# Statistics queued at other ticks, first products interleaved, last rows stored singly, and attention scores as three split-format matmuls

## The chip, the cores and the metric

The kernel runs on one core of a Trainium2 chip. The core has a matrix engine (TensorE, PE in the profile; its weight loads are shown as PEld), a vector engine (VectorE, DVE), a scalar engine (ScalarE, ACT), GpSimd (POOL) and SyncE (SP), which here only issues DMAs. Each engine takes its instructions in the order in which they stand, and waits on semaphores for others. The metric is the device time of one execution in microseconds (us); a median of several is given with their spread.

## The reference

One layer on 512 tokens of width 2048, all in float32. `rms_norm` divides by the root of the mean square over the features.

```python
xn = rms_norm(x, attn_norm_g[l])
proj = jnp.einsum("bsd,dc->bsc", xn, w_in[l])
u_val, u_gate, q, k, v = jnp.split(proj, split_pts, axis=-1)
y_conv = conformer_conv(u_val, u_gate, ...)   # GLU, conv of width 31, LayerNorm, silu
y_na = neighborhood_attention(heads(q), heads(k), heads(v), rpb[l])
mixed = jnp.concatenate([rms_norm(y_conv, conv_out_g[l]),
                         rms_norm(y_na, na_out_g[l])], axis=-1)
x = x + jnp.einsum("bsc,cd->bsd", mixed, w_out[l])
xn = rms_norm(x, ffn_norm_g[l])
up = jnp.einsum("bsd,df->bsf", xn, w_up[l])
up = depthwise_conv(up, ffn_dw_w[l], ffn_dw_b[l])
gate, val = jnp.split(up, 2, axis=-1)
x = x + jnp.einsum("bsf,fd->bsd", jax.nn.silu(gate) * val, w_down[l])
return rms_norm(x, final_norm_g)
```

The convolution and the attention have 1024 features each; the attention has 16 heads of 64, and each token of the 8 x 64 grid sees 8 x 16 neighbours. The gated MLP has 5632 hidden features.

## The kernel before

**Number format.** Activations lie with features on the 128 partitions and the 512 tokens along them. An fp32 operand is split in two fp32r parts, high and low: ACT copies the high part (`hi`), DVE subtracts it for the low one (`lo`). `mm3` makes one product of three fp32r matmuls: high by high, high by low, low by high. Weights come in units of 512 KB (eight blocks of 128 x 128): a DMA into `raw` (7 buffers), ACT to `whi` (L116), DVE to `wlo` (L117), with 4 buffers each. Every unit feeds 24 matmuls or so on PE. Not split are the attention's scores (`scores`, L449): q and k are fp32 there, and 64 partitions hold one head, so that a pair's two heads lie on the two halves of the array, taken in turn (j = 0, 1), for four blocks of tokens; the results go to four banks of two blocks each.

**Order.** The program is written as one stream, and a scheduler places each instruction by its place in the text, which `shifted` moves and `pin` fixes. Work that is to run beside a stream of products is written as generators in two lists, `steps` and `asteps`; `tick`, called after each unit of products, advances the first of each list by one `yield`. So a `yield` more or less in a generator moves the work behind it by one unit of products.

**Stages.** (1) A warm-up of PE (L231: two matmuls of 512 columns, three of 256, three of 224 on 128 rows; L235: four of 512 and eight of 256 columns on 64 rows, the two halves in turn), then the projections in an order given by `ORDER`: convolution inputs, v, and q and k per pair of heads. The depthwise convolution (`y`) runs on DVE. `attention` is a generator in `steps`: per pair of heads tables, scores, softmax, three yields, transposes on PE (`turn`, L476), and the product with v one pair later. `group_a` in `asteps`, begun at the fifth pair, is the convolution's LayerNorm: eight `ys` added (L371, L373), a matmul with ones for the mean (L376), subtraction and squares, the sum of squares (L185 in `rsqrt_steps`), then a second norm. (2) The output projection in two halves, `out_half(ma, ...)` and `out_half(mb, after)`; `after` sums into `x2`, writes it to DRAM with sums of squares, and makes of each two tiles seven combinations `comb` (`halves`, xc) for a Strassen product of two by two blocks. (3) `stats2` computes `rstd2` from those sums, in the steps of the first up products. `up_apart` (first four hidden tiles) and `up` make seven products (`pu`) each instead of eight, with weights added on DVE (`ws`); `hidden` does norm, convolution of width 3 and silu; `in_two` splits the hidden tile (hh, hl). `down` multiplies the tiles of the chunk before (`pend`) between products. Chunks are of four tiles, NCH = 11.

**rsqrt_steps.** Four one-column matmuls give column sums (st), DVE and ACT take them to 1/sqrt (rsv, rsr, rsy), DVE splits it (rsh, rsl) and makes diagonal matrices (dg), and after a `yield` PE multiplies dg with ones (L202), which spreads the result over partitions; ACT copies it from the bank (L206). Both banks have the tag "po" here, the one that `up_apart` takes for its seventh product.

**Tail.** For the last down products, three quarters of the tokens are done with features on partitions, and the last 128 tokens with tokens on partitions (`pt`). The former are normalised by `finish`, in pairs of tiles: each third pair on POOL, from a copy `rb` that ACT makes of the norm, the others on DVE; each pair is a store of 384 KB on SP's queue. The last 128 tokens (xg) are scaled and stored in four pieces (L932).

Of the kernel before, what the change touches and what calls it, by code (L numbers as in the profile page):

```python
# [10 lines left out]
F32 = mybir.dt.float32  # L11
# [5 lines left out]
P = 128  # L17
D = 2048
# [36 lines left out]
RA_AFTER = 5  # L55
# [12 lines left out]
def layer(ctx: ExitStack, tc: tile.TileContext, xT, xG, w_in, w_v, w_out, w_up, w_down, par, tab, g3, out, last_out):  # L68
# [110 lines left out]
    def rsqrt_steps(acc, n, name, to=slice(0, S), keep=True, by_token=None):  # L179

        m = (to.stop - to.start) // P
        ps = psa.tile([P, S], F32, tag="po", name="st")[:, :m]
# [16 lines left out]
        yield  # L199
        ps = psa.tile([P, S], F32, tag="po", name="st")[:, :m * P]  # L200
# [166 lines left out]
    def group_a():  # L367
        yield
        yield
        acc = t2("acc")  # L370
        nc.vector.tensor_add(acc, ys[0], ys[1])  # L371
        for i in range(2, NC_):
            nc.vector.tensor_add(acc, acc, ys[i])  # L373
        yield
        ps = psa.tile([P, S], F32, tag="po", name="st")
        nc.tensor.matmul(ps, ones, acc, start=True, stop=True)  # L376
# [27 lines left out]
    def project_qk(p):  # L404
        got = []
        for j, nm in enumerate("qk"):
# [9 lines left out]
            got.append(t)  # L416
# [25 lines left out]
    def scores(p, first):  # L442
# [4 lines left out]
        for b in range(NB):  # L447
            for j, hp in enumerate(hps):
                m = nc.tensor.matmul(banks[b // 2 * 2 + j][:, b % 2, :], q[hp, b * P:(b + 1) * P],  # L449
                                     keys(k, b)[hp], start=True, stop=True)  # L450
                if not first:
                    pin(m)
                first = False
# [139 lines left out]
    def after(d, ps):  # L593
# [10 lines left out]
        if d % 2 == 0:  # L604
            return
# [25 lines left out]
    def stats2():  # L631
# [5 lines left out]
        rstd2.append((yield from rsqrt_steps(acc2, D, "rstd2")))  # L637
# [117 lines left out]
    def up_apart(f, between):  # L755

        def product(c):
            w = weights()
            ps = (psa.tile([P, S], F32, tag="po", name="pu") if c == 6 else
                  psm.tile([P, S], F32, tag="mm", name="pu"))[:, :H]  # L760
            for k in range(U):
                m = comb[c][k]
                i = mm3(ps, w, k, m[:, :H], m[:, H:], k == 0, k == U - 1)
            tick(i)
# [56 lines left out]
    pend = None  # L821
    for c in range(NCH):
        hs = []
        for i in range(CH):
# [4 lines left out]
            hs.append(hidden(c * CH + i, lambda at: None if last else down(pend, down_units(c, i, at))))  # L829
        hs = [h if isinstance(h, tuple) else in_two(h) for h in hs]  # L830
# [35 lines left out]
    def finish(pair, r, apart):  # L866
# [10 lines left out]
        nc.sync.dma_start(out[pair], o)  # L877
# [30 lines left out]
    for g, ps in enumerate(banks):  # L908
# [11 lines left out]
        nc.vector.tensor_mul(xg[g], ps, gains[g])  # L920
# [6 lines left out]
    for g in range(CH):  # L927
        if g % 2:
# [78 lines left out]
```

## Time and profile before

| | us |
|---|---|
| median of 3 runs | 2038.44 (2037.53 to 2039.32) |
| the profiled execution | 2039.84 |
| its span, first to last instruction | 2038.1 |
| PE busy in it | 2021.4 |
| DVE, ACT, POOL busy | 1664.6, 1036.9, 159.7 |
| last matmul ends, about | 2028.7 |

The mean granted clock of PE is 0.998 of full speed. In the profile each line names engine, source line, operation and what it wrote and read, with buffer numbers left out: `pu<-xc,whi` is a product `pu` of activations `xc` and weights `whi`. A matmul's record is longer than the time after which the next starts (0.39 us for 512 columns, started every 0.23 us), so starts are compared rather than durations. "[1.32 <-DVE acc L373]" means that the engine stood idle for 1.32 us and that the wait was ended by DVE's work on line 373. A line of the windows has from:to in us, the length, for each of PE, PEld, DVE, ACT and POOL the busy us and the instruction count, then PE's granted clock, the DMA engines' busy share and GB/s.

### The profile page before, as it was taken

What the parts mean: (1) busy time and instruction counts of PE and PEld (TensorE: products, weight loads), DVE (VectorE), ACT (ScalarE), POOL (GpSimd) and SP (SyncE); (2) the same over time, 40 slices, a digit from 0 to 9 for tenths busy, and PEclk for the clock granted to TensorE, in tenths of its full rate; (3) what the DMA queues carried; (4) which work ended last, traced back from release to release, by engine and by line L of the source; (5) the groups of instructions that cost most, each with busy time, mean ns of one, the idle gap of its engine ahead of it and who ended that gap; (6) DMA issues with size and microseconds to landing.
All of it is one profiled execution on the core that took longest, in us unless ns stands there. A gap on an engine that the chain in (4) does not pass through costs nothing.

```text
span 2038.1 us, 28060 instructions
## 1 busy us (share of the span) xinstructions
PE 2021.4 (99%) x10608; PEld 1727.4 (85%) x10608; DVE 1664.6 (82%) x2278; ACT 1036.9 (51%) x1658; POOL 159.7 (8%) x188
## 2 busy tenths in 40 slices
PE   9999999999999999999999999999999999999998
PEld 7888888878888898888888888888888888888887
DVE  7986888878577898888888878888888888889875
ACT  7323234347345555555555555555555555555563
POOL 0000000000001001111111111111111111110111
PEclk9999999999999999999999999999999999999999
DMA  7233333336337445566565565566566566565583
GB/s 255 83 104 90 113 98 104 105 121 212 105 123 179 110 123 137 122 151 145 129 142 145 127 144 142 128 144 145 118 152 145 124 145 145 129 141 124 145 212 120
DMA packets 97063, 276.40 MB, mean 136 GB/s; under 512 B 10912, under 2 KB 11424, under 8 KB 96928
## 3 DMA queue, kind: packets, MB, share of 16 engines
q1 hardware_dynamic: 71568, 228.45, 36.6%
q0 software_dynamic: 25216, 46.15, 15.5%
q8 instruction: 84, 1.38, 0.3%
q14 instruction: 51, 0.42, 0.1%
q10 hardware_dynamic: 144, 0.01, 0.0%
HBM read 220.04 MB, written 54.53 MB: 135 GB/s over the span
## 4 chain that ended last, share of the span: by engine, by line
PE 95%; DVE 2%; ACT 1%; issue 1%; DMA 0%; ACTq 0%; DVEq 0%
PE pu L700 25%; PE pu L705 13%; PE pd L129 8%; PE pd L127 8%; PE pd L128 8%; PE pj L127 5%; PE pj L129 5%; PE pj L128 5%; PE po L127 3%; PE po L129 3%; PE po L128 3%; PE pv L307 1%; PE pv L309 1%; PE pv L308 1%; PE pu L127 1%; PE pu L128 1%
## 5 line engine op out<-in xcount | busy, mean ns | idle before, releaser
L116 ACT ACTIVATE whi<-raw 128x1024 fp32r<-128x1024 f32 x364 | 384.9, 1059 | 504.7 <-PE pj L128 147.7
L117 DVE TENSOR_TENSOR wlo<-raw,whi 128x1024 fp32r<-128x1024 f32 x364 | 443.9, 1220 | 215.4 <-ACT whi L116 205.7
L700 PE MATMUL pu<-xc,whi 128*128 128x512 f32 x2240 | 574.8, 392 | 0.9 <-ACT pl L712 0.9
L700 PEld LDWEIGHTS pu<-xc,whi 128*128 128x128 f32 x2240 | 409.1, 189 | 75.0 <-ACT pl L712 1.2
L705 PEld LDWEIGHTS pu<-xc,wlo 128*128 128x128 f32 x2240 | 305.6, 190 | 21.9
L705 PE MATMUL pu<-xc,wlo 128*128 128x256 f32 x2240 | 312.3, 282 | 0.0
L129 PE MATMUL pd<-hh,wlo 128*128 128x512 f32 x640 | 249.2, 391 | 0.0
L128 PE MATMUL pd<-hl,whi 128*128 128x512 f32 x640 | 249.2, 389 | 0.0
L127 PE MATMUL pd<-hh,whi 128*128 128x512 f32 x640 | 249.0, 391 | 0.0
L819 POOL DMA_DIRECT2D x2d<-pdc x160 | 139.6, 874 | 1167.6 <-ACT pdc L818 1053.8
L128 PE MATMUL pj<-xl,whi 128*128 128x512 f32 x512 | 200.4, 391 | 0.0
L129 PE MATMUL pj<-xh,wlo 128*128 128x512 f32 x512 | 200.2, 391 | 0.0
L127 PE MATMUL pj<-xh,whi 128*128 128x512 f32 x512 | 198.7, 392 | 0.0
L712 ACT ACTIVATE pl<-pu 128x256 f32<-128x256 f32 x280 | 104.4, 382 | 168.3 <-PE pu L700 168.2
L116 ACT ACTIVATE whi<-ws 128x1024 fp32r<-128x1024 f32 x132 | 139.7, 1059 | 76.8 <-PE pu L700 55.2
L361 DVE SCALAR_TENSOR_TENSOR y<-ch,prm,y 128x500 f32<-128x500 f32 (+14 forms) x240 | 173.4, 740 | 4.5
L117 DVE TENSOR_TENSOR wlo<-ws,whi 128x1024 fp32r<-128x1024 f32 x132 | 160.8, 1218 | 19.7 <-ACT whi L116 19.6
L129 PEld LDWEIGHTS pd<-hh,wlo 128*128 128x128 f32 x640 | 120.1, 188 | 28.8 <-DVE wlo L117 3.0
L128 PEld LDWEIGHTS pd<-hl,whi 128*128 128x128 f32 x640 | 120.2, 188 | 25.0
L127 PEld LDWEIGHTS pd<-hh,whi 128*128 128x128 f32 x640 | 120.5, 188 | 21.8
L818 ACT ACTIVATE pdc<-pd 128x512 f32<-128x512 f32 x160 | 93.8, 588 | 84.6 <-PE pd L129 84.5
L127 PEld LDWEIGHTS pj<-xh,whi 128*128 128x128 f32 x512 | 96.4, 188 | 21.3 <-issue 1.9
(197 smaller groups left out, 2851.5 us busy)
## 6 DMA issues: line engine op xcount, KB each, us to landing
raw<-in_w_up SPq DMA_DIRECT2D x176, 512.0 KB, 3.7
raw<-in_w_down SPq DMA_DIRECT2D x88, 512.0 KB, 3.9
x2d<-pdc POOLq DMA_DIRECT2D x160, 256.0 KB, 4.8
raw<-in_w_in SPq DMA_DIRECT2D x60, 512.0 KB, 3.7
raw<-in_w_out SPq DMA_DIRECT2D x32, 512.0 KB, 3.7
raw<-in_w_v SPq DMA_DIRECT2D x16, 512.0 KB, 4.0
tab<-in_tab SPq DMA_DIRECT2D x32, 256.0 KB, 4.9
x<-in_xG SPq DMA_DIRECT2D x16, 256.0 KB, 5.4
```

Of the source, the lines that this page charges most:

```text
L116: i = nc.scalar.activation(hi[:, :n], raw[:, :n], AF.Copy)
L117: j = nc.vector.tensor_sub(lo[:, :n], raw[:, :n], hi[:, :n].bitcast(F32))
L127: nc.tensor.matmul(ps, hi[:, a], mh, start=start, stop=False)
L128: nc.tensor.matmul(ps, hi[:, a], ml, start=False, stop=False)
L129: return nc.tensor.matmul(ps, lo[:, a], mh, start=False, stop=stop)
L307: nc.tensor.matmul(ps, xh, wh[:, f], start=kk == 0, stop=False)
L361: nc.vector.scalar_tensor_tensor(y[:, a:b], h[:, a + j - PAD:b + j - PAD], prm[:, o + j:o + j + 1], y[:, a:b], op0=ALU.mult, op1=ALU.add)
L700: return nc.tensor.matmul(ps, w[0][:, k * P:(k + 1) * P], comb[c][k], start=k == 0, stop=k == U - 1)
L705: nc.tensor.matmul(ps[:, H:], w[1][:, k * P:(k + 1) * P], comb[c][k][:, :H], start=False, stop=False)
L712: nc.scalar.activation(to, ps, AF.Copy)
L818: nc.scalar.activation(t, ps, AF.Copy)
L819: nc.gpsimd.dma_start(xd[d], t, accum_op=ALU.add)
```

## The change

Seven edits in one function. The scores become three fp32r matmuls of q's and k's parts, which `project_qk`'s end now splits. `group_a` begins two ticks earlier, has a yield among its subtractions, sums the second norm's squares in the loop that makes the tiles, with yields there, and has `RA_AFTER` 2 instead of 5. `stats2` is queued two ticks later, rests twice and takes the bank "sc". The combination of the last two tiles is given an earlier place (`combine`), and the first two up products are written as seven blocks of each, then the last block of each. The last hidden tile of the chunk before the last is split behind the fourth product of the next tile. The first pair of the tail is normalised on DVE from the bank and stored as two halves before `rb` is copied, and the last piece of xg is scaled in one step.

```diff
-RA_AFTER = 5
+RA_AFTER = 2
...
-    def rsqrt_steps(acc, n, name, to=slice(0, S), keep=True, by_token=None):
+    def rsqrt_steps(acc, n, name, to=slice(0, S), keep=True, by_token=None, free=False, rest=1):
+
+        def bank():
+            if free:
+                return psa.tile([P, 2, S], F32, tag="sc", name="st")[:, 0]
+            return psa.tile([P, S], F32, tag="po", name="st")
...
-        yield
-        ps = psa.tile([P, S], F32, tag="po", name="st")[:, :m * P]
+        for _ in range(rest):
+            yield
+        ps = bank()[:, :m * P]
...
     def group_a():
-        yield
-        yield
         acc = t2("acc")
...
             sum_sq(acc, ys[i], i == 0)
+            if i == NC_ // 2 - 1:
+                yield
         yield
         yield
         r = yield from rsqrt_steps(acc, CONV, "rln")
...
             ma.append(split(ys[i], pc("cog", i), "ma"))
-        for i in range(NC_):
             sum_sq(acc, ys[i], i == 0)
+            if i % 2:
+                yield
         for _ in range(RA_AFTER):
             yield
...
-            got.append(t)
+            h, l = t2(nm + "h", F32R), t2(nm + "l", F32R)
+            nc.scalar.activation(h, t, AF.Copy)
+            nc.vector.tensor_sub(l, t, h.bitcast(F32))
+            got.append((h, l))
...
-            for j, hp in enumerate(hps):
-                m = nc.tensor.matmul(banks[b // 2 * 2 + j][:, b % 2, :], q[hp, b * P:(b + 1) * P],
-                                     keys(k, b)[hp], start=True, stop=True)
+            at = slice(b * P, (b + 1) * P)
+            for part, (x, y) in enumerate(((0, 0), (0, 1), (1, 0))):
+                for j, hp in enumerate(hps):
+                    m = nc.tensor.matmul(banks[b // 2 * 2 + j][:, b % 2, :], q[x][hp, at], keys(k[y], b)[hp],
+                                         start=part == 0, stop=part == 2)
...
-        if d % 2 == 0:
-            return
+        if d % 2:
+            with shifted(-200 if d == KD - 1 else 0):
+                combine(d)
+
+    def combine(d):
...
-        rstd2.append((yield from rsqrt_steps(acc2, D, "rstd2")))
+        yield
+        yield
+        rstd2.append((yield from rsqrt_steps(acc2, D, "rstd2", free=True, rest=2)))
...
+        def first_two():
+            got = [begin(c) for c in range(2)]
+            for c in range(2):
+                tick(part(c, *got[c], range(U - 1)))
+            for c in range(2):
+                part(c, *got[c], range(U - 1, U))
+            return [ps for _, ps in got]
...
-        for i in range(2):
-            nc.scalar.activation(vv[:, i], product(i), AF.Copy)
+        for i, ps in enumerate(first_two() if f == 0 else map(product, range(2))):
+            nc.scalar.activation(vv[:, i], ps, AF.Copy)
...
+    def behind(c, i, at):
+        if c == NCH - 1 and (i, at) == (0, 3):
+            pend[-1] = in_two(pend[-1])
+        down(pend, down_units(c, i, at))
...
-        hs = [h if isinstance(h, tuple) else in_two(h) for h in hs]
+        if c != NCH - 2:
+            hs = [h if isinstance(h, tuple) else in_two(h) for h in hs]
...
-    def finish(pair, r, apart):
+    def finish(pair, r, apart=False, split=False):
...
-        nc.sync.dma_start(out[pair], o)
+            if split:
+                nc.sync.dma_start(out[pair][:, i], o[:, i])
+        if not split:
+            nc.sync.dma_start(out[pair], o)
...
+            finish(pairs.pop(0), rb[0], split=True)
             rb.append(t2("rb")[:, fm])
             nc.scalar.activation(rb[1], rb[0], AF.Copy)
...
-        nc.vector.tensor_mul(xg[g], ps, gains[g])
+        if g < CH - 1:
+            nc.vector.tensor_mul(xg[g], ps, gains[g])
...
-        if g % 2:
+        if g == CH - 1:
+            nc.vector.scalar_tensor_tensor(xg[g], banks[g], y, gains[g], op0=ALU.mult, op1=ALU.mult)
+        elif g:
             nc.scalar.activation(xg[g], xg[g], AF.Copy, scale=y)
```

The change moves instructions on DVE and ACT at three places. First DVE at the convolution's mean, where `acc` sums the eight tiles `y`, `tab` is the softmax of a pair, `wlo` a weight unit, and `mu` the mean read from PE's result. Before:

```order
L373 TENSOR_TENSOR acc<-acc,y 128x512
L466 TENSOR_TENSOR tab<-tab,su 128x512
L373 TENSOR_TENSOR acc<-acc,y 128x512
L117 TENSOR_TENSOR wlo<-raw,whi 128x1024
L465 RECIPROCAL su<-su 128x2
L373 TENSOR_TENSOR acc<-acc,y 128x512
L466 TENSOR_TENSOR tab<-tab,su 128x512
L373 TENSOR_TENSOR acc<-acc,y 128x512 x2
L117 TENSOR_TENSOR wlo<-raw,whi 128x1024
L378 TENSOR_SCALAR mu<-st 128x512
```

With the change:

```order
L367 TENSOR_SCALAR y<-ch,prm,y 128x497
L117 TENSOR_TENSOR wlo<-raw,whi 128x1024
L375 TENSOR_TENSOR acc<-y 128x512
L377 TENSOR_TENSOR acc<-acc,y 128x512 x6
L117 TENSOR_TENSOR wlo<-raw,whi 128x1024
L382 TENSOR_SCALAR mu<-st 128x512
L385 TENSOR_TENSOR y<-y,mu 128x512 x4
L170 TENSOR_TENSOR acc<-acc,sq 128x512
L416 TENSOR_TENSOR q<-pj,rstd_530 128x512
L170 TENSOR_TENSOR acc<-acc,sq 128x512
L385 TENSOR_TENSOR y<-y,mu 128x512
L170 TENSOR_TENSOR acc<-acc,sq 128x512
```

The additions (L373, now L375 and L377) stood among the softmax's steps; they now stand in one block behind the last tap of the convolution (L367), and the softmax stands behind some of the subtractions (L385).

Second, DVE in `stats2`, from the read of the column sums to the diagonal matrices. Before:

```order
L187 TENSOR_SCALAR rsv<-st 128x4
L117 TENSOR_TENSOR wlo<-ws,whi 128x1024
L174 RECIPROCAL rsr<-rsr 128x4
L117 TENSOR_TENSOR wlo<-raw,whi 128x1024
L175 TENSOR_SCALAR rsy<-rsr 128x4
L176 TENSOR_TENSOR rsy<-rsy,rsv 128x4
L177 TENSOR_SCALAR rsy<-rsy,rsr 128x4
L192 COPY rsh<-rsy 128x4
L193 TENSOR_TENSOR rsl<-rsy,rsh 128x4
L197 TENSOR_TENSOR dg<-ident,rsh 128x512
L197 TENSOR_TENSOR dg<-ident,rsl 128x512
```

With the change, from the reciprocal on (one more `wlo` operation stands between `rsv` and it, and the second dg follows the last row):

```order
L174 RECIPROCAL rsr<-rsr 128x4
L117 TENSOR_TENSOR wlo<-raw,whi 128x1024
L175 TENSOR_SCALAR rsy<-rsr 128x4
L117 TENSOR_TENSOR wlo<-ws,whi 128x1024
L176 TENSOR_TENSOR rsy<-rsy,rsv 128x4
L673 TENSOR_TENSOR ws<-ws,raw 128x1024
L177 TENSOR_SCALAR rsy<-rsy,rsr 128x4
L117 TENSOR_TENSOR wlo<-raw,whi 128x1024
L197 COPY rsh<-rsy 128x4
L666 TENSOR_TENSOR ws<-raw 128x1024
L198 TENSOR_TENSOR rsl<-rsy,rsh 128x4
L202 TENSOR_TENSOR dg<-ident,rsh 128x512
```

Two operations of 128x1024 stood within the chain before; six do now, with L666 and L673 adding weight blocks. On PE 71 product matmuls stand between the column sums and the matmul with dg, where 28 stood.

Third, ACT at the start of the last chunk. `uy` and `hh` belong to the last hidden tile of the chunk before, `vv` and `pl` are copies of the next tile's products. Before:

```order
L786 ACTIVATE uy<-g,prm 128x512
L786 ACTIVATE uy<-vl,prm,fwn 128x512
L116 ACTIVATE whi<-ws 128x1024
L797 ACTIVATE uy<-uy 128x512
L116 ACTIVATE whi<-raw 128x1024
L803 ACTIVATE hh<-uy 128x512
L712 ACTIVATE vv<-pu 128x256
L712 ACTIVATE pl<-pu 128x256
L712 ACTIVATE vv<-pu 128x256
L712 ACTIVATE pl<-pu 128x256 x2
```

With the change:

```order
L815 ACTIVATE uy<-g,prm 128x512
L815 ACTIVATE uy<-vl,prm,fwn 128x512
L728 ACTIVATE vv<-pu 128x256
L728 ACTIVATE pl<-pu 128x256
L116 ACTIVATE whi<-ws 128x1024
L826 ACTIVATE uy<-uy 128x512
L728 ACTIVATE vv<-pu 128x256
L728 ACTIVATE pl<-pu 128x256
L116 ACTIVATE whi<-raw 128x1024
L728 ACTIVATE pl<-pu 128x256
L832 ACTIVATE hh<-uy 128x512
```

The copy to `hh` stood ahead of the products' copies; it now stands behind the first five of them.

More of the change, by code (lines that the diff above doesn't have):

```diff
@@ L755, in up_apart, with begin, part, product @@
     def up_apart(f, between):
[L757 to L761, printed above, removed]
+        def begin(c):
+            return weights(), (psa.tile([P, S], F32, tag="po", name="pu") if c == 6 else
+                               psm.tile([P, S], F32, tag="mm", name="pu"))[:, :H]
+        def part(c, w, ps, ks):
+            for k in ks:
                 m = comb[c][k]
                 i = mm3(ps, w, k, m[:, :H], m[:, H:], k == 0, k == U - 1)
-            tick(i)
+            return i
+        def product(c):
+            w, ps = begin(c)
+            tick(part(c, w, ps, range(U)))
             between(c)
             return ps
+        def first_two():
[5 more added lines that the diff above has]
+            return [ps for _, ps in got]
         vv, v, uu, g = (t2(n).rearrange("p (i t) -> p i t", i=2) for n in ("vv", "vl", "uu", "g"))
         both = lambda x: x.unsqueeze(1).broadcast_to([P, 2, H])
-        for i in range(2):
-            nc.scalar.activation(vv[:, i], product(i), AF.Copy)
+        for i, ps in enumerate(first_two() if f == 0 else map(product, range(2))):
+            nc.scalar.activation(vv[:, i], ps, AF.Copy)
         u, u2 = uu[:, 0], uu[:, 1]
@@ L828, in layer @@
                 hs = [in_two(h) for h in hs]
-            hs.append(hidden(c * CH + i, lambda at: None if last else down(pend, down_units(c, i, at))))
-        hs = [h if isinstance(h, tuple) else in_two(h) for h in hs]
+            hs.append(hidden(c * CH + i, lambda at: None if last else behind(c, i, at)))
+        if c != NCH - 2:
+            hs = [h if isinstance(h, tuple) else in_two(h) for h in hs]
         if not last:
```

8 lines of the change are left out of this document (4 added, 4 removed).

## The prediction

> **What bounds the kernel now.** I read the page's first two parts first: who is busy, and in what clock.
>
> ```profile
> PE 2021.4 (99%) x10608; PEld 1727.4 (85%) x10608; DVE 1664.6 (82%) x2278; ACT 1036.9 (51%) x1658; POOL 159.7 (8%) x188
> ```
>
> TensorE (PE) is busy 2021.4 of 2038.1 us. No engine can make this kernel shorter but PE, and an edit can gain in three ways only: less matmul time, fewer of PE's waits, or a shorter tail after the last matmul. So the second view is the list of PE's waits (engine, line, what it waited for; us in total, times, longest).
>
> ```profile
> PE st L376 <- DVE acc L373: 1.3, 1, 1.3
> PE st L202 <- DVE dg L197: 1.1, 1, 1.1
> PE trp L476 <- DVE tab L466: 0.9, 1, 0.9
> PE pu L700 <- ACT pl L712: 0.9, 1, 0.9
> PE pu L127 <- ACT rstd L206: 0.7, 1, 0.7
> PE pu L127 <- ACT xc L589: 0.6, 1, 0.6
> ```
>
> Six waits, 5.5 us together, each met once. In starts from one matmul to the next each costs some 0.16 us more than the list says, since a record ends after the next could have started; about 6.9 us lie here. The third view, the windows, shows the clock PE was granted around the second and fifth of them (busy us and count of PE, PEld, DVE, ACT, POOL; then PEclk).
>
> ```profile
> 686.60:690.00 3.40, 3.40 (x28) 3.21 (x27) 2.97 (x7) 1.16 (x3) 0.00 (x0) 1.00 0.66 192
> 690.00:693.50 3.50, 1.64 (x8) 1.03 (x8) 3.43 (x7) 1.93 (x3) 0.00 (x0) 1.00 0.32 118
> 693.50:696.90 3.40, 3.40 (x18) 3.40 (x17) 2.84 (x5) 0.00 (x0) 0.00 (x0) 0.50 0.00 0
> 431.50:434.90 3.40, 2.08 (x8) 1.13 (x7) 3.22 (x5) 1.06 (x1) 0.00 (x0) 1.00 0.53 154
> ```
>
> After PE sat idle for 1.86 of 3.50 us, it ran at half clock for 3.4 us: 18 matmuls where 28 had fitted before the wait, so 10 x 0.121 = 1.2 us lost. After the 1.32 us idle in 431.5:434.9 nothing of the kind follows. What can be gained from waits and clock is thus 8.1 us, 0.4% of the time.
>
> **The change, part by part.** *Scores (eight pairs).* Removed are 8 fp32 matmuls a pair, added 24 fp32r ones of the same shape.
>
> ```profile
> 237.04 1.60 PEld L449 LDWEIGHTS sc<-k,q 64*128 64x128 f32 x16 [0.35 <-issue]
> 237.04 2.00 PE L449 MATMUL sc<-k,q 64*128 64x256 f32 x16
> 238.97 0.50 PE L127 MATMUL pj<-xh,whi 128*128 128x512 f32 x1
> 1.64 2.48 PE L231 MATMUL idle<-warm 128*128 128x512 f32 x8 [1.64 <-DVE warm L228]
> 4.05 2.08 PE L235 MATMUL idle<-warm 64*128 64x512 f32 x12
> 679.81 0.28 PE L128 MATMUL pu<-xc,whi 128*128 128x256 f32 x1
> 679.93 0.29 PE L129 MATMUL pu<-xc,wlo 128*128 128x256 f32 x1
> ```
>
> One pair's scores take 238.97 - 237.04 = 1.93 us now, for 16 records (an fp32 matmul leaves two). Do two 64-row fp32r matmuls on different halves of the array run side by side? The warm-up has both kinds. L231's eight 128-row matmuls stream, by the code and its groups, 2 x 512 + 3 x 256 + 3 x 224 = 2464 columns from 1.64 to 4.05, 0.98 ns a column. L235's twelve 64-row ones, alternating halves as the scores do, stream 4 x 512 + 8 x 256 = 4096 columns in 2.00 us (the next matmul starts at 6.05), 0.49 ns. So they do. A pair of the new matmuls therefore takes one slot, and a 256-column fp32r slot is 679.93 - 679.81 = 0.12 us: 12 slots are 1.44 us, plus the 0.2 us that I give to changing formats at both ends (the 0.32 us to the next start at entry, against 0.23 in a row of projections), 1.64. That is 0.29 x 8 = **-2.3 us**. Bounds: slots at the rate of the present ones (1.93 / 8 = 0.24 us for two passes of 256 columns, so 0.11) give 1.5 us, -3.4 in all; loads that don't run side by side (24 x 0.10 us, from 1.60 / 16) give 2.4 us, +3.8; matmuls one after the other 24 x 0.12 + 0.2 = 3.1 us, +9.2. I take the slot, since a 128-row matmul with a load of its own already keeps it.
>
> The Trainium skill speaks against this edit ("TensorE: Matmul & The Clock Gate", Part 3, row/col tiling): a weight load overlaps matmuls in flight only when it goes to other rows of the array. By that rule every load would wait for its own half's last matmul. The 0.12 us rows at 679.8 don't bear it out: there each load goes to the rows that are computing.
>
> The split also adds 16 copies on ACT and 16 subtractions on DVE, of the form of these rows:
>
> ```profile
> L803 ACT ACTIVATE hh<-uy 128x512 fp32r<-128x512 f32 x44 | 27.2, 621 | 10.2 <-DVE uy L798 10.2
> L804 DVE TENSOR_TENSOR hl<-uy,hh 128x512 fp32r<-128x512 f32 x44 | 30.1, 683 | 0.7 <-ACT hh L803 0.7
> 240.00:420.00 180.00, 180.00 (x945) 148.20 (x945) 142.25 (x206) 70.14 (x126) 0.00 (x0) 1.00 0.34 106
> 420.00:440.00 20.00, 18.68 (x86) 14.60 (x83) 19.61 (x34) 9.17 (x24) 0.00 (x0) 1.00 0.27 79
> 460.00:480.00 20.00, 19.09 (x90) 15.55 (x88) 18.91 (x34) 19.30 (x39) 0.00 (x0) 1.00 0.33 106
> ```
>
> 10 us on each engine. In 240:420 DVE has 38 us idle and ACT 110, which hides five pairs for nothing. In 420:440 and 460:480 DVE has 0.4 and 1.1 us left: there the cover is gone, and what two pairs add, 4 x 0.68 = 2.7 us, is the price if all of it shows.
>
> *The convolution's statistics.* The mean's seven additions now stand in one block behind the last tap, ahead of the softmax they were mixed with. So the wait of L376 goes:
>
> ```profile
> 431.48 0.39 PE L129 MATMUL pj<-xh,wlo 128*128 128x512 f32 x1
> 431.71 0.39 PE L127 MATMUL pj<-xh,whi 128*128 128x512 f32 x1
> 433.41 1.10 PE L376 MATMUL st<-acc,ones 128*128 128x512 f32 x2 [1.32 <-DVE acc L373]
> ```
>
> 433.41 - 431.71 - 0.23 = 1.48 us. Late next is the matmul that sums the squares (L190 after). Until it, PE has 68 projection matmuls x 0.227, 16 short ones of the attention (some 0.12 each) and one pair's scores, 15.4 + 1.9 + 1.6 = 19 us. DVE has 8 subtractions, 9 additions of squares, q's two steps and one pair's softmax, 31 operations of 0.6 us from start to start and a few small ones: 19 us, and half a microsecond to begin. A tie, so a new wait: I take 0.9 (0 to 1.5 or, with the softmax late, 2). **-0.6 us**, bounds -1.5 and +0.5. The sums of squares of the second norm only move into cover.
>
> *Wait of trp L476.* It stands at 479.56, behind softmax steps on a full DVE and ACT. The second norm's steps leave this stretch, the split's come in; half of 1.07 us goes, **-0.5**, bounds -1.1 and +1.3 (one pair's 2 x 0.68).
>
> *First products interleaved.* PE's order of the first 92 matmuls of this product pair is the same before and after: the scheduler had already put them so. The combination of the last two tiles keeps its place on DVE too. The 0.6 us wait for xc (0.78 in starts) stays: **0**; if something shifts, -0.8 or +0.4.
>
> *Statistics of x2.* Two ticks later, two rests, and another bank.
>
> ```profile
> 690.32 0.68 DVE L197 TENSOR_TENSOR dg<-ident,rsh 128x512 fp32r<-128x512 f32 x1
> 690.92 0.68 DVE L197 TENSOR_TENSOR dg<-ident,rsl 128x512 fp32r<-128x512 f32 x1
> 691.15 1.01 PE L202 MATMUL st<-dg,ones 128*128 128x512 f32 x2 [1.13 <-DVE dg L197]
> 692.85 0.39 PE L127 MATMUL pu<-xc,whi 128*128 128x256 f32 x1 [0.69 <-ACT rstd L206]
> L117 DVE TENSOR_TENSOR wlo<-ws,whi 128x1024 fp32r<-128x1024 f32 x132 | 160.8, 1218 | 19.7 <-ACT whi L116 19.6
> ```
>
> The wait for rstd came from the product that took the same bank; with a bank of its own it goes. For dg, PE now has 71 matmuls x 0.12 = 8.5 us of cover, where it had 28. But DVE's order puts six 1.22 us operations between the chain's small ones (7.3 us), and with seven of about 0.1 us and two dg of 0.6 the chain takes 9.2, plus some 0.7 for the start and the square root on ACT: a wait of 1.4. In starts the place costs 2.5 now, so **-1.0**, bounds -2.5 and +0.5.
>
> *Clock.* With one wait of 1.4 us in place of two of 1.86 idle, PE's idle is as at 431.5, where no drop followed: **-1.2**, bounds -1.2 and 0. The Trainium skill ("TensorE: Matmul & The Clock Gate", Part 1) says that the gate looks at free-running windows of 3.4 us, so the same idle may or may not halve the clock, by where it falls. The 3.4 us of the half clock agree with that; by this rule the term is a chance, not a sum, and the third rival below prices its loss.
>
> *in_two moved behind the next hidden's start.*
>
> ```profile
> 1864.57 1.04 ACT L116 ACTIVATE whi<-raw 128x1024 fp32r<-128x1024 f32 x1
> 1866.37 0.63 ACT L803 ACTIVATE hh<-uy 128x512 fp32r<-128x512 f32 x1 [0.76 <-DVE uy L798]
> 1866.91 0.36 ACT L712 ACTIVATE vv<-pu 128x256 f32<-128x256 f32 x1
> ```
>
> ACT stood 0.76 us at hh with the copies of products behind it, and PE waited for their banks. Now the copies stand first, and hh comes when its input is long there; nothing waits for hh until the down products read it. The wait of L700 goes: **-1.1**, bounds -1.1 and 0.
>
> *Tail.*
>
> ```profile
> 2022.12 0.49 ACT L903 ACTIVATE rb<-st 128x384 f32<-128x384 f32 x1 [2.64 <-PE st L202]
> 2022.65 3.76 DVE L876 SCALAR_TENSOR_TENSOR fin<-x,prm,st 128x384 f32<-128x384 f32 x7 [1.57 <-ACT rb L903]
> 2024.72 6.27 SPq L877 DMA_DIRECT2D out_T<-fin  x8
> 2024.00:2036.00 12.00, 4.69 (x22) 3.49 (x20) 7.59 (x20) 3.49 (x9) 4.64 (x5) 0.81 0.89 342
> DMA packets 1728, 4.20 MB, mean 280 GB/s; under 512 B 192, under 2 KB 192, under 8 KB 1728
> ```
>
> The end is set by 4.2 MB of output at some 390 GB/s, 10.7 us from the first transfer of 2024.72. Two stores of 0.2 MB now go out near 2022.8 and 2023.3. But the copy rb now stands behind both DVE rows of the first pair, so POOL starts 1.1 us later, and SP, in order, holds its third store for POOL until about 2025.8 where the first was 2024.72. The 0.4 MB sent early are worth 1.0 us and the later start costs 1.1: **+0.1**, bounds -0.6 and +0.6. The last rows' fused step saves DVE and ACT work that the drain hides.
>
> **Sum.** -2.3 - 0.6 - 0.5 + 0 - 1.0 - 1.2 - 1.1 + 0.1 = -6.6 us. On the profiled span of 2038.1 us that is 2031.5. Its own execution took 2039.84 us, 1.4 above the median of 2038.44, so I put the sum on the median: 2031.8, **2032**.
>
> **Rivals.** *The score matmuls do not run side by side* (slower side). Place: the scores' slots in eight pairs; price +9.2 in place of -2.3, so -6.6 + 11.5 = +4.9, **2043.3**. The edit itself loses from (1.93 - 0.2) / 12 = 0.144 us a slot on, the whole change from 0.19, where a pair's scores take 0.54 us longer than now. For it: in the warm-up no three products are summed in one bank; against: the 0.49 ns a column. *DVE full at 420 to 480*: the 2.7 us of the added subtractions show on PE, at L190 and the transposes, and half of what was gained there is lost (+1.1): -6.6 + 3.8 = -2.8, **2035.6**. For it the 19.61 of 20 us; against it that the sums move ahead, towards the stretch where DVE has its 38 us idle. *The clock drop stays* where dg waits: **2033**. *The interleaving and the tail do not do what they say*: already in the sum at 0 and +0.1; if they do, 0.8 + 0.6 better, **2030.5**.
>
> **How the numbers follow.** Forecast 0.52, clock drop stays 0.20, DVE full 0.12, side by side fails 0.08, better by the two edits 0.08. The likeliest one's own range is 2030 to 2034. The range of 2029 to 2036 leaves out the slower rival (0.08) and some 0.1 of misjudged terms. A measurement of this kernel tells about 0.2% from no change, 4.1 us: faster is below 2034.4, slower above 2042.5. Forecast, clock and better edits are faster with 0.80 less a little of their upper ends, and I give 0.79; same 0.13 (DVE full and those ends); slower 0.08.
>
> **What would show it.** In the changed profile a pair's scores should take 1.5 to 1.8 us with starts in pairs; over 1.93 and the first rival holds. The list of waits should have no mean matmul (L380), no pu behind pl and none behind rstd, but one each of st for the column sums below 1.5 us, of trp, of xc (0.6) and of dg (about 1.3). PEclk should stay 1.00 around 690. On ACT at 1866 two copies should stand ahead of uy. The first store should go out before 2024 on the old clock of events (some 6.5 us earlier in all), with a gap after the second, and the transfers should still end the span. The prediction is wrong if PE's waits together exceed 4 us, or if the scores gain nothing.

## The result and the profile after

The changed kernel takes 2032.72 us (median of 9 runs, 2032.04 to 2036.41) against 2038.43 us before (9 runs, 2037.53 to 2039.4): a ratio of 0.9973, 95% interval 0.9965 to 0.9981. Predicted were 2032.0. The profiled execution took 2032.23 us, with a span of 2030.3 where before had 2038.1. So the two spans lie 7.8 us apart, the medians 5.7; the section on the prediction comes back to that.

The page's busy times, and the list of PE's waits after the change (engine, line, what it waited for; us in total, times, longest):

```profile
PE 2016.6 (99%) x10672; PEld 1726.0 (85%) x10672; DVE 1673.5 (82%) x2293; ACT 1045.7 (52%) x1674; POOL 159.7 (8%) x188
```

```profile
PE st L208 <- DVE dg L202: 1.5, 1, 1.5
PE pu L127 <- ACT xc L600: 0.8, 1, 0.8
PE st L190 <- DVE acc L170: 0.3, 1, 0.3
```

Three waits, 2.6 us together, are left of six with 5.5. Gone are the waits for the mean (for acc, L373 before), for trp, for rstd and for pl; new is the one at the column sums; the wait for dg is a little longer in one piece. The first pair's scores, from the timeline of PE (start, us, what, count):

```profile
237.00 0.39 PE L460 MATMUL sc<-kh,qh 64*128 64x256 f32 x2
237.22 0.29 PE L460 MATMUL sc<-kl,qh 64*128 64x256 f32 x2
...
238.40 0.29 PE L460 MATMUL sc<-kh,ql 64*128 64x256 f32 x2
238.62 0.50 PE L127 MATMUL pj<-xh,whi 128*128 128x512 f32 x1
```

Each row of `sc` is two matmuls that start less than 0.02 us apart, one on each half of the array, and the rows follow each other at 0.12 us: 238.62 - 237.00 = 1.62 us a pair, where it was 1.93. The windows (busy us and count of PE, PEld, DVE, ACT, POOL; then PEclk) of the two crowded stretches, and around the wait for dg:

```profile
420.00:440.00 20.00, 19.68 (x97) 16.27 (x96) 19.17 (x38) 12.29 (x29) 0.00 (x0) 1.00 0.26 77
460.00:480.00 20.00, 20.00 (x101) 16.66 (x100) 16.75 (x30) 14.98 (x33) 0.00 (x0) 1.00 0.49 153
690.00:693.50 3.50, 2.05 (x16) 1.83 (x16) 3.50 (x7) 1.33 (x2) 0.00 (x0) 1.00 0.42 133
693.50:696.90 3.40, 3.40 (x30) 3.36 (x30) 3.40 (x7) 1.08 (x2) 0.00 (x0) 1.00 0.33 82
```

DVE, which was full in 420:440 and nearly so in 460:480, now has 0.8 and 3.3 us left although the split added to its work: the mean's additions left the first of these stretches, and of the second norm some of the work left the other (four of its eight steps for `mal` and four of its seven sums are still there). After the wait for dg no half clock follows: 30 matmuls in 3.4 us where before had 18.

The tail of the changed kernel: SP's stores, POOL's first results, and the transfers' rate in forty slices of 2014 to 2031.

```profile
2014.91 0.87 SPq L914 DMA_DIRECT2D out_T<-fin  x2
2018.03 5.28 SPq L916 DMA_DIRECT2D out_T<-fin  x7
2016.01 5.88 POOL L910 TENSOR_TENSOR fin<-x,rb 128x384 f32<-128x384 f32 x6 [39.02 <-ACT rb L943]
GB/s 0 0 0 0 304 362 260 0 0 0 0 210 419 383 398 398 383 419 383 412 376 405 405 383 419 369 419 369 390 381 381 386 366 386 106 0 0 0 0 0
```

Two small stores go out early, then the transfers stand still for four slices, 1.7 us, until POOL's pair is stored at 2018.03. From the last matmul to the end it takes 9.5 us, 9.4 before.

### The profile page after: what moved, and what is told of

Read it like the earlier page. It is cut to its first block, busy times and chain, and to the rows that moved or that the text cites. A ratio compares the mean times of both kernels' runs of the same rounds, so it can differ in the third digit from the quotient of the medians.

```text
span 2030.3 us, 28220 instructions
## 1 busy us (share of the span) xinstructions
PE 2016.6 (99%) x10672; PEld 1726.0 (85%) x10672; DVE 1673.5 (82%) x2293; ACT 1045.7 (52%) x1674; POOL 159.7 (8%) x188
## 4 chain that ended last, share of the span: by engine, by line
PE 97%; DVE 2%; issue 0%; ACT 0%; DMA 0%; ACTq 0%; DVEq 0%
PE pu L716 25%; PE pu L721 13%; PE pd L129 8%; PE pd L127 8%; PE pd L128 8%; PE pj L127 6%; PE pj L129 5%; PE pj L128 5%; PE po L127 3%; PE po L128 3%; PE po L129 3%; PE pv L313 1%; PE pv L315 1%; PE pv L314 1%; PE pu L127 1%; PE pu L128 1%
## 5 line engine op out<-in xcount | busy, mean ns | idle before, releaser
L367 DVE SCALAR_TENSOR_TENSOR y<-ch,prm,y 128x500 f32<-128x500 f32 (+14 forms) x240 | 173.5, 742 | 4.3
```

The source lines that it names most:

```text
L367: nc.vector.scalar_tensor_tensor(y[:, a:b], h[:, a + j - PAD:b + j - PAD], prm[:, o + j:o + j + 1], y[:, a:b], op0=ALU.mult, op1=ALU.add)
```

## The experiments

Twelve kernels ran; where there are several runs the time is their median. Each had the kernel before beside it, at 2038.79 to 2038.92, which is 0.4 to 0.5 us more than the 2038.43 beside the changed kernel; so differences to the changed kernel's 2032.72 carry that much doubt. A profile shows one execution.

**The split scores alone**, on the kernel before.

```diff
-                m = nc.tensor.matmul(banks[b // 2 * 2 + j][:, b % 2, :], q[hp, b * P:(b + 1) * P],
-                                     keys(k, b)[hp], start=True, stop=True)
+            for part, (x, y) in enumerate(((0, 0), (0, 1), (1, 0))):
+                for j, hp in enumerate(hps):
+                    m = nc.tensor.matmul(banks[b // 2 * 2 + j][:, b % 2, :], q[x][hp, at], keys(k[y], b)[hp],
+                                         start=part == 0, stop=part == 2)
...
```

(and the split of q and k as in the change.)

> The kernel before with the split scores alone. Theory (a pair of 64-row fp32r matmuls takes one slot of 0.12 us, and the added copies and subtractions find room): 1.62 us a pair in place of 1.93, 8 x 0.31 = 2.5 us less, 2036.0 at a median of 2038.4 before, with the six waits of before still there (5.5 us in the list, give or take 1). Rival (DVE is full at 420 to 480, where before left it 0.4 and 1.1 us of 20): the waits for acc and tab grow by up to 2.7 us, and the time stays at 2038.

Measured: 2041.2 us (11 runs, 2038.77 to 2045.41), ratio 1.0011 (1.0003 to 1.002): no gain, but a small loss. Its profile is that of the slowest of the eleven executions (2045.41), so that a wait in it need not be in the others. PE's waits there:

```profile
PE pu L127 <- ACT xc L594: 3.8, 1, 3.8
...
PE po L127 <- DVE oa L580: 1.4, 1, 1.4
PE st L202 <- ACT ao L502: 1.4, 1, 1.4
...
PE st L376 <- DVE acc L373: 1.0, 1, 1.0
PE pu L705 <- ACT pl L717: 0.8, 1, 0.8
```

Neither theory had this. The wait for acc fell by 0.3 and that for trp went, but two waits of 1.4 us stand at 501 to 505, and the wait for xc has grown from 0.6 to 3.8; DVE stood 8.3 us for loads of weights between 560 and 690 us, 1.7 in the changed kernel (more on this below). The spread of the second norm (st L202, a bank of "po") waits for the copy ao that frees its bank, and the first sums with the norm (oa) are late behind it. Both stood in this order before, without a wait. What comes late is the softmax of the seventh pair, and with it all that DVE and ACT do behind it: its first step stood 2.24 us for the pair's tables. SP's issue of these tables before, here and in the changed kernel, and that step here:

```profile
484.03 1.81 SPq L437 DMA_DIRECT2D tab<-in_tab  x4
486.78 2.12 SPq L440 DMA_DIRECT2D tab<-in_tab  x4
475.32 1.89 SPq L446 DMA_DIRECT2D tab<-in_tab  x4
493.02 1.37 DVE L464 SCALAR_TENSOR_TENSOR tab<-sc,tab 128x512 f32<-128x512 f32 x2 [2.24 <-DMA tab<-in_tab]
```

Here they stand on SP behind two more weight loads than before, and these go out as DVE frees their buffers; in the changed kernel they go out 12 us ahead of the pair's scores. Before had no wait for a table. So the late tables are what the trace shows ahead of the two waits; no run moved the tables alone.

**The halves of the array apart.** Same matmuls, one head's twelve behind the other's.

```diff
-        for b in range(NB):
-            ...
-                for j, hp in enumerate(hps):
+        for j, hp in enumerate(hps):
+            for b in range(NB):
```

> The changed kernel with its score matmuls in another order: all twelve of one head, then all twelve of the other, so that no two neighbours lie on different halves of the array. Theory (the gain rests on the two halves working side by side): 24 x 0.12 + 0.2 = 3.1 us a pair in place of 1.62, 8 x 1.46 = 11.7 us more in the span, 2042. Rival (the format alone gains, the halves don't matter): 1.6 us a pair, span as after, 2030.

Measured: one execution of 2040.1 us, its span 2038.0, 7.7 over the changed kernel's. The first pair:

```profile
237.49 0.38 PE L460 MATMUL sc<-kh,qh 64*128 64x256 f32 x1
...
238.54 0.28 PE L460 MATMUL sc<-kh,ql 64*128 64x256 f32 x1
238.55 0.39 PE L460 MATMUL sc<-kh,qh 64*128 64x256 f32 x2
238.77 0.28 PE L460 MATMUL sc<-kl,qh 64*128 64x256 f32 x2
238.89 0.28 PE L460 MATMUL sc<-kh,ql 64*128 64x256 f32 x2
...
240.17 0.50 PE L127 MATMUL pj<-xh,whi 128*128 128x512 f32 x1
```

240.17 - 237.49 = 2.68 us: 21 slots of 0.12 and 0.2 around them. Single rows keep the 0.12 us that a double row takes, so the gain does rest on the halves working side by side. The theory had 24 slots; three rows in the middle are double (see the last section). 8 x 1.06 = 8.5 us, less what the longer cover saved at L190 and xc.

**group_a undone**, all other edits kept.

```diff
     def group_a():
+        yield
+        yield
...
-            if i == NC_ // 2 - 1:
-                yield
...
+        for i in range(NC_):
             sum_sq(acc, ys[i], i == 0)
-            if i % 2:
-                yield
```

(RA_AFTER = 5 again.)

> The changed kernel with the edits of group_a undone (yields and RA_AFTER = 5 as before). Theory, from the run of the scores alone (where two new waits of 1.4 us stood at 501 to 503, for ao and oa): the split's extra DVE and ACT work pushes the old second norm into the last pair's softmax, and the edits of group_a are what clears it; so here the wait for acc at the mean comes back (1.0 to 1.5 us) and waits of 2 to 3 us stand near 500, and the time is 3 to 4 us over 2032.7. Rival (the two waits at 501 were of another origin): the mean's wait alone, at most 1.2 us more, 2033.9.

Measured: 2039.26 us (10 runs, 2038.52 to 2043.72), 6.5 over the changed kernel (6.1 when each is taken against the kernel before beside it). The waits came back as forecast, and cost more:

```profile
PE pu L127 <- ACT xc L600: 3.3, 1, 3.3
...
PE po L127 <- DVE oa L586: 1.4, 1, 1.4
PE st L208 <- ACT ao L508: 1.4, 1, 1.4
PE st L382 <- DVE acc L379: 1.0, 1, 1.0
```

3.1 us in starts at 500, 1.1 at the mean, and 2.6 more for xc, in an execution 1.6 us above the median. That the edits of group_a clear these waits is shown by this pair of kernels. That the added work on DVE and ACT makes them, as the theory has it, is not: here too the softmax stood for its tables (1.5 us, issued at 486.06).

**The stores of x2 off SP's queue**, with group_a undone: what makes the wait for xc so long?

```diff
-        nc.sync.dma_start(xd[d], x2[d])
+        nc.scalar.dma_start(xd[d], x2[d])
```

> The kernel with the edits of group_a undone, and the 16 stores of x2 issued by ACT and not by SP. Theory (a loop: SP's weight load stands behind the store of x2, the store waits for DVE's x, x stands on DVE behind the sum of weights, and that sum waits for the load; once late by a product it stays late): without the stores on SP the load comes early, the wait for xc falls from 3.3 us to under 0.5, and with it the half clock behind it, so the span falls from 2039.1 to about 2035; the two waits of 1.4 us near 500 stay. Rival (the transfers themselves are late because the DMA engines are full there): the wait for xc stays over 2 us.

```profile
PE pu L127 <- ACT xc L600: 0.4, 1, 0.4
```

Measured: one execution of 2038.21 us. The two waits of 1.4 us at 500 stay, the one for xc falls from 3.3 to 0.4, and the span from 2039.1 to 2036.4; the 2035 of the theory were not reached, as this execution has a half clock of its own at 504 (last section). DVE stood 8.0 us for loads of weights in 560 to 690 us with the stores on SP, and 0.8 with them on ACT. PE's order is the same in both kernels, and DVE's but for two sums of weights that stand one row earlier. The half clock that followed the long wait (granted clock 0.76 and 0.74 in 681.4 to 688.2) went with it.

The loop of the theory is not what the rows show, though. With the stores on SP, ahead of the long wait:

```profile
673.16 1.22 DVE L117 TENSOR_TENSOR wlo<-raw,whi 128x1024 fp32r<-128x1024 f32 x1
674.41 0.33 SPq L111 DMA_DIRECT2D raw<-in_w_up  x1
678.87 1.22 DVE L668 TENSOR_TENSOR raw<-raw 128x1024 f32<-128x1024 f32 x1 [2.75 <-DMA raw<-in_w_up]
```

The load goes out 0.03 us after the `wlo` that frees its buffer (674.38), and so does every weight load from 590 to 682, in both kernels: none was held back by a store. What differs is how long the loads take. From issue to landing in 600 to 682 (last number, median in us), with the stores on SP and then on ACT:

```profile
raw<-in_w_up SPq DMA_DIRECT2D x8, 512.0 KB, 6.7
raw<-in_w_up SPq DMA_DIRECT2D x8, 512.0 KB, 4.2
```

So DVE stood for loads that landed late, and with the stores on another queue they landed sooner, in one execution of each kernel. Why they landed late, and whether they do in every execution, is not shown.

**The scores and group_a together**, on the kernel before.

> The kernel before with the split scores and the edits of group_a, all else as before. Theory (these two belong together; with the split alone two waits of 1.4 us near 501 and one of 3.8 us for xc came up, and the edits clear all three): -2.5 for the scores, -1.5 for the mean, -1.1 for trp, +0.5 for the column sums, so some 4.5 us under the kernel before, 2034.2, with the waits for dg, rstd and pl as before. Rival (what cleared them is in another edit): the waits at 501 or the xc wait of over 2 us stay, 2037 or more.

Measured: 2034.9 us (10 runs, 2033.43 to 2036.08), ratio 0.9981 (0.9972 to 0.999): the theory. No wait near 500 or for trp; dg 1.1 and rstd 0.7 as before, xc 0.8 (0.6 before), pl 0.3, and 0.3 at the column sums. So of the 5.7 us between the medians, these two edits bring about 4. The windows where before had its half clock, 3.5 us earlier here:

```profile
686.60:690.00 3.40, 1.63 (x7) 1.04 (x8) 3.37 (x7) 1.80 (x3) 0.00 (x0) 1.00 0.33 123
690.00:693.50 3.50, 3.50 (x31) 3.50 (x30) 3.22 (x7) 0.45 (x1) 0.00 (x0) 1.00 0.00 0
```

1.77 us idle of 3.4, the same waits as before's 1.86, and the clock stays whole.

**The fp32 scores in the changed kernel.**

```diff
-            h, l = t2(nm + "h", F32R), t2(nm + "l", F32R)
-            nc.scalar.activation(h, t, AF.Copy)
-            nc.vector.tensor_sub(l, t, h.bitcast(F32))
-            got.append((h, l))
+            got.append(t)
```

(and the one matmul of before.)

> The changed kernel with fp32 scores, unsplit, as before; all other edits kept. Theory (the split gains 0.31 us a pair and nothing else, once the edits of group_a make room): 2.5 us more, span 2033.1, 2035.2 in the runs, no new wait on PE. Rival (the edits of group_a only work with the split's order): waits of 1 us or more near 430 to 505, 2036.5 or more.

Measured: 2034.59 us (10 runs, 2034.13 to 2035.4), 1.9 over the changed kernel's median, span 2033.5 (the slowest of the ten), no new wait, and none at the column sums. By the rows the split gives 2.5 us and takes back the 0.5 us of the wait at the column sums, 2.0 in all, which is the 1.9 measured; taken against the kernel before beside each it is 1.4. With the old group_a it lost 2.4.

**stats2: the bank without the delay, and the delay without the bank.**

```diff
-        yield
-        yield
-        rstd2.append((yield from rsqrt_steps(acc2, D, "rstd2", free=True, rest=2)))
+        rstd2.append((yield from rsqrt_steps(acc2, D, "rstd2", free=True)))
```

> The changed kernel with stats2 queued and rested as before, but with the bank sc kept. Theory (the bank removes the wait for rstd, and the later queueing buys little, since what it adds to PE's cover it adds to DVE's chain): one wait for dg of 1.4 to 2 us in all, none for rstd, span within 0.5 us of the changed kernel's 2030.6. Rival (the delay is what shortens the wait): 2.7 us or more for dg, span 1.1 us longer.

```diff
-        rstd2.append((yield from rsqrt_steps(acc2, D, "rstd2", free=True, rest=2)))
+        rstd2.append((yield from rsqrt_steps(acc2, D, "rstd2", rest=2)))
```

> The changed kernel with stats2 late and with two rests, but in the bank po as before. Theory (the product that takes the same bank waits for rstd's copy): the wait for rstd of 0.7 us or more is back, besides one of 1.4 us or more for dg; the sum at this place is 2.4 us or more in starts, where the changed kernel has 1.6. Rival (late enough, the bank collides with nothing): 1.6 us, span 2030.6.

Both theories fell. With the bank alone, one execution of 2037.55 us; no wait for dg at all, but these three:

```profile
PE st L190 <- DVE acc L650: 2.1, 1, 2.1
...
PE pu L127 <- ACT whi L116: 0.7, 1, 0.7
PE pu L129 <- DVE wlo L117: 0.5, 1, 0.5
```

The bank sc is free sooner, and the column sums stand 25 matmuls earlier on PE than in the changed kernel, ahead of the moment when acc2 has come back from DRAM and been added: what the delay is for. With the delay alone, one execution of 2038.93 us:

```profile
PE st L208 <- DVE dg L202: 4.3, 1, 4.3
```

The bank po is needed by the seventh product, so the matmul with dg must come ahead of it: 47 matmuls behind the column sums in place of 71. 24 x 0.12 = 2.9 us less cover, and the wait is 2.9 us longer in starts. The wait for rstd did not come back. In both kernels a half clock follows (0.50 in one window of 3.4 us, parts of two others). In these two executions each half of the edit alone loses 5.5 and 6.9 us in the span, of which the half clock can be up to 3.4 (the deficits of the windows: 0.22, 0.50 and 0.28 of 3.4 us with the bank alone). The waits themselves are longer than the changed kernel's in both, so the two belong together.

**in_two undone.**

```diff
-        if c == NCH - 1 and (i, at) == (0, 3):
-            pend[-1] = in_two(pend[-1])
...
-        if c != NCH - 2:
+        if True:
             hs = [h if isinstance(h, tuple) else in_two(h) for h in hs]
```

> The changed kernel with in_two of the last hidden tile back in its old place. Theory (ACT stands at hh with the products' copies behind it): PE's wait for pl of 0.9 us is back near 1858, span 1.06 us longer, 2031.6. Rival (that wait came from a late transfer alone): no wait there, 2030.6.

```profile
PE pu L716 <- ACT pl L728: 0.3, 1, 0.3
```

Measured: one execution of 2032.75 us, span 2030.6. Between the two: the wait is back, but with 0.3 us, 0.44 in starts, not 0.9. ACT's order does cost something, and how much hangs on when a load of weights lands that DVE needs ahead of the steps for hh. Before and here:

```profile
1859.59 1.23 DVE L652 TENSOR_TENSOR raw<-raw 128x1024 f32<-128x1024 f32 x1 [1.53 <-DMA raw<-in_w_up]
1852.04 1.23 DVE L668 TENSOR_TENSOR raw<-raw 128x1024 f32<-128x1024 f32 x1 [0.91 <-DMA raw<-in_w_up]
```

The step came 4.3 us after SP had issued the load (1855.30) before, and 3.7 us here (1848.36); hh follows 6.8 us later in both. So 0.6 us of before's wait are this load. But with the old place the wait was 0.8 in the list with the split scores alone (1.0 in starts), where the load took 3.75 us and was issued half a microsecond later against PE, and 0.3 (0.48) with scores and group_a. It thus lay between 0.44 and 1.06 us in four profiles.

**The products' edits undone.**

```diff
-            with shifted(-200 if d == KD - 1 else 0):
+            with shifted(0):
                 combine(d)
...
-        for i, ps in enumerate(first_two() if f == 0 else map(product, range(2))):
+        for i, ps in enumerate(map(product, range(2))):
```

> The changed kernel with the two edits at the first up products undone (combination of the last two tiles at its old place, products one after the other in the text). Theory (neither moves an instruction): 2032.7, within 0.5, PE's wait for xc 0.8 us in the list as after. Rival (they act): that wait is 0.3 us or more away from 0.8. Two of nine executions after stood at 2036.4; if the clock gate's windows decide, single executions here stand some 1.5 us or a multiple above the lowest too.

Measured: 2032.57 us (8 runs, 2032.16 to 2035.44), span 2030.6, the wait for xc 0.6 us. The instructions of this kernel stand in the same order as the changed kernel's on every engine, so this is a second measurement of the same program: the difference between 0.6 and 0.8 is the scatter of that wait, and a single high execution (2035.44) came here too.

**The tail's stores in another order.**

```diff
-    pairs = list(range(KD // 2))
+    pairs = [0, 2, 1, 3, 5, 4, 6, 7]
```

with the stores kept in the order of the text.

> The changed kernel with the stores of the tail in the order 0, 2, 1, 3, 5, 4, 6, 7 of the pairs, so that the third store waits for DVE and not for POOL. Theory (the transfers end the span, and they stand still from 2016.7 to 2018.9 because SP waits for POOL's pair until 2018.03, while DVE's pair is there at about 2017.2): the third store goes out 0.8 us earlier, and the time from the last matmul to the end falls from 9.5 to about 8.7 us, 2031.9 for 2032.7. Rival (the last 128 tokens' pieces end the span, their last store at 2026.65): no change, 9.5 us.

```profile
2014.62 0.87 SPq L914 DMA_DIRECT2D out_T<-fin  x2
2016.85 5.29 SPq L916 DMA_DIRECT2D out_T<-fin  x7
```

Measured: 2031.89 us (5 runs, 2031.06 to 2033.48). The third store goes out 2.2 us behind the first in place of 3.1, and the time from the last matmul to the end is 8.6 us in place of 9.5. The theory holds in the profile, 0.9 us. The medians lie 0.8 apart in the same direction, but the runs overlap, so the time alone does not show it.

**That order, and the x2 stores on ACT's queue.**

> The changed kernel with the stores of the tail in the order 0, 2, 1, 3, 5, 4, 6, 7 and the 16 stores of x2 on ACT's queue. Theory (the same loop holds the 0.6 to 0.9 us wait for xc, and its late mode makes the executions at 2036): the wait for xc is under 0.3 us, 2031.2 in the median against 2031.9 for the stores' order alone, and no execution over 2033. Rival (the wait for xc is DVE's own chain): the wait stays at 0.6 or more, 2031.9.

```profile
PE pu L127 <- ACT xc L600: 0.8, 1, 0.8
```

Measured: 2031.73 us (5 runs, 2031.12 to 2032.31), ratio to before 0.9964 (0.9951 to 0.9978), the fastest kernel of the study, though its runs overlap with those of the stores' order alone. The wait for xc did not go, so here the stores do not make it. The rival is not shown either, as DVE stood 0.6 us for the weights' load at 672 here as in the changed kernel. No execution was above 2033, but five runs are too few to say that none would be.

## Why the prediction was right

The time was right within 0.7 us: 2032.0 forecast, 2032.7 measured, or -6.6 by the sum against -5.7 between the medians. By its own steps:

*Scores, -2.3.* Right: 1.62 us a pair for 1.64 predicted, 0.31 x 8 = 2.5. The bound on the halves was settled by taking them apart. The Trainium skill's rule ("TensorE: Matmul & The Clock Gate", Part 3), that a weight load overlaps only with matmuls on other rows, does not describe this trace: with the halves apart every load but those around the change of halves went to the rows that were computing, and the slot stayed 0.12 us.

*group_a, -0.6.* On the path it gave 1.48 less 0.48 in starts, -1.0, as the wait at the column sums was 0.48 and not the 0.9 of the tie. But the step costed the edit against the waits of the kernel before. Undone beside the split scores it costs some 6 us. The rival "DVE full at 420 to 480" comes nearest to the result without this edit, but neither of its places showed: the waits came at 500 and for xc, not at L190 or the transposes, and the traces have DVE standing for late transfers ahead of both. The prediction had no term for what an edit does to the order and the landing of transfers.

*trp, -0.5.* The whole 1.07 went. *Products, 0.* Right: 0.92 in starts for 0.78, the same program. *Tail, +0.1.* Right in size and cause: 9.5 us for 9.4, and the order of the stores shows what held it.

*Statistics of x2, -1.0.* Right in sum: 1.6 in starts for 2.5, a wait of 1.45 us for the 1.4 forecast. The reasons were half right: the prediction took bank and delay as two gains that add up, and each alone is a loss.

*in_two, -1.1.* Mis-sized: the wait went in the profile, but undone the edit gave 0.44 us back. The 1.06 of before's profile hold 0.6 us of a load that took longer there, so the term is 0.44 to 1.06 by the execution.

*Clock, -1.2.* Here the sum was right for the profile, and the medians do not bear it out. Before's profiled execution (2039.84) lies above all its nine runs of the comparison (at most 2039.4; of 18 runs beside the first experiments three were higher). It is 1.4 us above their median, and the changed kernel's profiled execution 0.5 below its own: that makes most of the 2.1 us between the two differences. Before's profile holds the half clock and the late load, about 1.2 and 0.6 us, that need not be in the others: the kernel with scores and group_a had the same two waits, and no half clock. That these two are the 1.4 us is likely but not shown, as before has one profile only. The Trainium skill (same page, Part 1) has the gate look at windows that run free of the kernel, by which the same idle may or may not halve the clock; the two cases agree with that. The prediction counted as a sum what it had just called a chance. That this did not show in the time is luck: trp, group_a and the scores gave 1.2 more than forecast.

The spans, in starts: scores -2.5, group_a -1.0, trp -1.1, xc +0.1, stats2 -0.9, clock -1.2, pl -1.1, tail +0.1: -7.6 of 7.8.

What stays open: two of nine executions of the changed kernel stood at 2036.4, and one of the same program at 2035.44; none of these was profiled. A late xc as with group_a undone (2.6 us) with a half clock behind it would give that, but it wasn't seen in this kernel.

## What to carry to other kernels

An edit that adds work to a stage with idle time can still lose: the split scores gained only beside the edit of group_a, so undo edits one at a time from the end as well as adding them from the start. Where an engine stands late, follow the load that it waits for back to its issue, and see whether it went out late (the tables, behind two loads that waited for buffers) or took long (the weights, 6.7 us in place of 4.2); a story of queues that fits the times can still miss which. And a term that hangs on the phase of the clock, or on one transfer in one profile, belongs in the range and not in the sum.

## What the hardware showed that I had not expected

With the halves apart the program has twelve matmuls of one head and then twelve of the other. In the rows above, the second head's first matmul starts at 238.55, when three of the first head's are still to come; three slots hold two each. The rows do not name the half, but the trace's semaphore updates fit this order alone: they come from the 15th, 18th and 24th matmul in order of start (238.90, 239.25 and 239.97), which are then the first head's last, the second head's sixth and its last, where their banks are done. So a matmul for the idle half started ahead of three that stood before it for the busy half: on PE instructions need not start in the order in which they stand.

A wait's effect on the clock was not set by its length alone: 1.86 us idle in 3.5 us halved the clock in before's profile, 1.77 in 3.4 did not in the kernel with scores and group_a. The two waits near 500 show it more plainly, as PE runs the same instructions there with group_a undone (first two rows) and with the stores moved as well (last two):

```profile
500.66:504.06 3.40, 0.86 (x3) 0.30 (x2) 2.89 (x4) 2.70 (x4) 0.00 (x0) 1.00 1.05 387
504.06:507.46 3.40, 3.13 (x14) 2.61 (x15) 3.31 (x6) 0.00 (x0) 0.00 (x0) 1.00 0.97 379
500.90:504.30 3.40, 0.85 (x3) 0.30 (x2) 3.34 (x6) 2.70 (x4) 0.00 (x0) 1.00 1.05 386
504.30:507.70 3.40, 3.13 (x7) 2.48 (x8) 3.31 (x6) 0.00 (x0) 0.00 (x0) 0.50 0.98 380
```

PE stood 2.5 us in 3.4 in both, and then made 14 matmuls in 3.4 us in one and 7 in the other.
